# One fused decoder layer on one core: turned blocks stored whole, decays in two halves, exchanged banks, a third q,k buffer

## The chip, the core and the metric

The kernel runs on one core of a Trainium2 chip. The metric is the time of one execution on the device in microseconds (us). Three timed runs of the kernel before gave 1155.07, 1157.92 and 1158.22 us, so the median is 1157.92 us. One further execution was recorded by the profiler; all durations below are from it.

## What is computed

One decoder layer for 1024 rows of 1024 columns, in float32. With `h` the normed input, one projection gives q, k, v, z_a, a low-rank gate, four convolution inputs and two merge gates. Cut to what matters here:

```python
gk  = log_sigmoid(gk_low @ w_gk2 + b_gk) / 16          # decays
o   = gla_chunked(q, k, v, gk)                         # o_t = q_t S_t ; S_t = exp(gk_t) S_{t-1} + k_t^T v_t
y_a = (rms_norm(o, gla_norm_g) * silu(z_a)) @ w_branch_a
y_c = (cb * causal_dwconv(cc * xc) * silu(z_c)) @ w_branch_c
merged = sigmoid(g_a + b_ga) * y_a + sigmoid(g_c + b_gc) * y_c
x = x + merged @ w_out
x = x + sigmoid(rms_norm(x) @ w_ple_gate) * (p @ w_ple_proj)
out = rms_norm(x)
```

There are 4 heads with 128 key columns and 256 value columns, in chunks of 64 rows.

## The kernel before, in words

**Products.** Every float32 operand is split into a rounded high part and a low remainder, and a product is three matmuls (`mm3`, L604). The large products are 2 by 2 block products with seven block multiplications instead of eight (products 0 to 6, banks called X, Y and V). A `Cell` (L721) is one such product on one column block of weights; `wide` (L1061) is the form for v and z_a, with four banks at a time: X on `first`, V on `second`, Y on `first` again (L1120). The fourth bank of each four is one of two rotating buffers under the tag `o`, which other work uses too. `resident` (L637) splits the operand that stays in SBUF, one of seven slots `r0` to `r6`.

**Order.** Nothing is issued at once. `Flow.note` (L271) records every operation with a modelled cost, `set_dues` (L368) works out due times backwards, and `put_in_order` (L415) places the operations one by one: on each engine the one that can start first, by due time where several can. Large matmuls go in the order of the program; matmuls of side work (decays, attention) go in between as soon as their data are modelled to be there. What comes out is a fixed order for each engine, and an engine waits at an instruction whose data are late. All DMAs go out on SP's queue, in order. Buffers of one tag are handed out in program order; a pool made `instead` of another opens when the old one's last user is done. Side work is written as generators woven in by `weave` and `tick` (L612 to L623): a generator is resumed after so many ticks, two ticks for each four k-tiles.

**Stages, in the order of time.** Preparation of h and the first gate products; v and the decays; z_a; q and k; the convolution products; the gates (`ga`, `gc`) with the attention woven in; `yc`; `ya`; `out`; the last gate `gt` with the output.

- *Decays* (`decays`, L1169): a generator that runs beside v. For each half of the rows: a low-rank product into an `o` buffer, then for each head a matmul `zp` into an `o` buffer, then exp, log, a subtraction and a scan on tile `c` (tag `c4`, 2 buffers), stored as `cd`.
- *q, k* (`q_cons`, `k_cons`): scaled q and k go to DRAM (`qkd`). One k form is transposed in 32 by 32 blocks into `turned` and stored by `put_blocks` (L864) with four DMAs of 32 partitions each, so that DRAM holds the finished transpose (`ked`).
- *Attention* (`attend`, L1378): for each pair of heads eight row blocks and one closing step. A step's matmuls are one bundle: the state's growth `kv` and the output `op` of block s-1, then the scores `X` of block s. The loads of block s+1 (`fetch`, L1392: `qk`, `v`, `sz`, each behind its reader) come after step s; `qk` and `v` have two buffers each. `read_attended` (L1432) norms `op`, multiplies by `sz`, transposes, and after four blocks stores `od`, again by four DMAs.
- *Reload* (`switch`, L1492): the conv result `ud` and the attention result `od` are loaded (`uq`, `oq`) and split into resident operands. Pool `sw`, in which `uq` lies, opens `instead` of the attention's pool `att`.
- *Out and gate*: `flip` (L1600) transposes each half row block of x and stores it as `gd`, four DMAs each; `gt` cells load it as `raw`.

Of the kernel before, what the change touches and what calls it, by code (L numbers as in the profile page):

```python
# [49 lines left out]
class View:  # L50
# [88 lines left out]
    def place(self):  # L139
        real = self.buf.get()  # L140
        if self.apart:
            start, dims = self.apart
            return bass.AP(tensor=real.tensor, offset=real.offset + start,
                           ap=[[self.buf.size, 32]] + [[s, n] for s, n in dims])
# [113 lines left out]
class Flow:  # L258
# [12 lines left out]
    def note(self, engine, op, call, args, kw):  # L271
# [28 lines left out]
        elif engine == ACT:  # L300
            o.cost = 0.10 + n * 0.000833 + (0.1 if "accum_out" in kw else 0.0)
            o.table = TABLE.get(args[2] if len(args) > 2 else None, 0)
        elif engine == POOL:
            o.cost = 0.1 + n * 0.001 if op == "memset" else 0.6
        else:
            o.cost, o.bytes = 0.4, shape[0] * n * 4
            o.lat = 2.0 + o.bytes / 250e3
# [206 lines left out]
def kernel(  # L514
# [42 lines left out]
    vec = cp.tile([P, 62], F32, name="vec")  # L557
# [8 lines left out]
    ggla = vec[:, 60:62]  # L566
# [10 lines left out]
    ked = [[dram(f"ked{hp}_{i}", 2, 4 * P) for i in range(2)] for hp in range(2)]  # L577
# [9 lines left out]
    gd = [[dram(f"gd{p}_{q}", 2, 4, P) for q in range(2)] for p in range(4)]  # L587
# [49 lines left out]
    def resident(name, k, src):  # L637
        hi, lo = slot(k, "h", f"{name}{k}hi"), slot(k, "l", f"{name}{k}lo")
        for c in range(2):
            cs = slice(2 * c, 2 * c + 2)  # L640
            split(hi[:, cs, :], lo[:, cs, :], src[:, cs, :])
# [222 lines left out]
    def put_blocks(dst, start, dims, src):  # L864

        store(dst.spread(start, dims), src)


# [192 lines left out]
    def wide(name, w, pool, cons):  # L1061
# [49 lines left out]
        def copies(what, acc, tags):  # L1111
            out = []
            for b in range(4):
                where, tag = tags[b]
                t = where.tile([P, 512], F32, tag=tag, name=f"{name}{what}{b}", bufs=2)
# [4 lines left out]
        first, second = ("m0", "m1", "m2", "o"), ("m3", "m4", "m5", "o")  # L1120
        near = [(bp, "u2"), (bp, "u2"), (bp, "s5"), (bp, "s5")]
# [4 lines left out]
        x0 = copies("x", X, near)  # L1126
# [10 lines left out]
        c22 = copies("s", V, [(bp, "s5"), (bp, "s5"), (pool, "ws"), (pool, "ws")])  # L1137
        prep(5)
        product(2, Y, False)
        c12 = copies("u", Y, [(bp, "u2"), (bp, "u2"), (pool, "wu"), (pool, "wu")])  # L1140
# [14 lines left out]
    with phase("v", [ph["prep0"]]) as qp:  # L1155
# [13 lines left out]
        def decays():  # L1169

            smask = qp.tile([P, HALF], F32, name="smask")
            nc.gpsimd.memset(smask, 1.0)
            nc.gpsimd.memset(smask.rearrange("p (c t) -> p c t", t=CH)[:, :, 0:1], 0.0)
            graw = qp.tile([P, 8, 16], F32, name="graw")
            load(graw, wgl)
            gdif = qp.tile([P, 4, 16], F32, name="gdif")
            tt(gdif, graw[:, 4:8, :], graw[:, 0:4, :], op=ALU.subtract)


            glw = qp.tile([P, 12, 4, 32], F32R, name="glw")  # L1180
            for i in range(4):
                split(glw[:, 0:8, i, 0:16], glw[:, 0:8, i, 16:32], graw)
                split(glw[:, 8:12, i, 0:16], glw[:, 8:12, i, 16:32], gdif)
            g2raw = qp.tile([P, 512], F32, tag="low", name="g2raw")
            load(g2raw, wgk2)
            g2 = qp.tile([P, 512], F32R, name="g2")
            nc.scalar.copy(g2, g2raw)
            tt(g2[64:128], g2raw[64:128], f(g2[64:128]), op=ALU.subtract)
            yield 1
            for half in range(2):  # L1190

                ops = ((0, 0), (4, 3)) if half == 0 else ((0, 1), (8, 6))
                lowp = pso.tile([P, 512], F32, tag="o", name=f"lowp{half}", bufs=2)
                n = 0
                for g0, k in ops:
                    for kt in range(4):
                        gl = glw[:, g0 + kt, :, :].rearrange("p a b -> p (a b)")
                        for s in range(2):
                            mm(lowp, gl, hres[k][s][:, kt, :], start=n == 0, stop=n == 15)
                            n += 1  # L1200
                low = qp.tile([P, 512], F32R, tag="low", name=f"low{half}")
                nc.scalar.copy(low, lowp)
                for a in (32, 96):
                    tt(low[a:a + 32], lowp[a:a + 32], f(low[a:a + 32]), op=ALU.subtract)
                yield 1
                for hp in range(2):
                    t1 = qp.tile([P, 2, HALF], F32, tag="t1", name=f"t1_{half}{hp}")
                    c = [qp.tile([P, HALF], F32, tag="c4", name=f"c4_{half}{hp}{i}", bufs=2) for i in range(2)]
                    for i in range(2):
                        h = 2 * hp + i  # L1210
                        zp = pso.tile([P, 512], F32, tag="o", name=f"zp{half}_{h}", bufs=2)
                        cs = slice(h * P, (h + 1) * P)
                        mm(zp, g2[:, cs], low, start=True, stop=True)
                        act(t1[:, i, :], zp, AF.Abs, bias=bgk[:, h:h + 1])
                        nc.vector.tensor_scalar(c[i], zp, bgk[:, h:h + 1], 0.0, op0=ALU.add, op1=ALU.min)
                        yield 1
                    act(t1, t1, AF.Exp, scale=-1.0)
                    act(t1, t1, AF.Ln, bias=1.0)
                    for i in range(2):
                        tt(t1[:, i, :], t1[:, i, :], c[i], op=ALU.subtract)  # L1220
                        nc.vector.tensor_tensor_scan(c[i], smask, t1[:, i, :], 0.0, op0=ALU.mult, op1=ALU.add)
                        store(cd[2 * hp + i][half], c[i])
# [11 lines left out]
    with phase("qk", [ph["v"]]) as qp:  # L1234
# [36 lines left out]
        def k_cons(hp):  # L1271

            def cons(i, j, src):
# [104 lines left out]
    def attend(hp, ap):  # L1378
# [7 lines left out]
        ins, turns, aTs = {}, {}, {}  # L1386
        kes = slot(3, "h", f"ke{hp}", (2, 2, 512), F32)
        for i in range(2):
            load(kes[:, i], ked[hp][i])
        vb, qb = slot(0, "h", f"v{hp}", (2, 1024)), slot(0, "l", f"qk{hp}", (2, 1024))  # L1390

        def fetch(s):  # L1392
            v = vb[:, s % 2].rearrange("p (h l d) -> p h l d", h=2, l=2)
            qk = qb[:, s % 2].rearrange("p (h c) -> p h c", h=2)
            load(f(qk), qkd[hp][s // NP][:, s % NP])
# [8 lines left out]
            ins[s] = qk, v, sz, ke  # L1404

        def grow(s, kv):
            v = ins[s][1]
            for h in range(2):
                mm3(kv[:, h], *(k[:, h] for k in ins[s][3]), v[:, h, 0], v[:, h, 1], True, True)

        def attended(s, op):
            qk, v = ins[s][0:2]
# [19 lines left out]
        def read_attended(s, op):  # L1432
            sz = ins.pop(s)[2]
# [5 lines left out]
            nc.gpsimd.tensor_tensor(r, r, mhalf[:, 0:1].to_broadcast([P, 2]), op=ALU.pow)  # L1439
            for h in range(2):  # L1440
                stt(sz[:, h], op[:, h], r[:, h:h + 1], sz[:, h], op0=ALU.mult, op1=ALU.mult)
# [9 lines left out]
        for s in range(2):  # L1451
            fetch(s)
        yield 2
        for s in range(n + 1):
# [8 lines left out]
            if X:  # L1463
                qk = f(ins[s][0])
# [9 lines left out]
            if s and s + 1 < n:  # L1474
                fetch(s + 1)
            yield 3
# [15 lines left out]
    def switch(cell, name, side, pool, src, res, bufs=3, gain=None):  # L1492


        def get(n):
            t = pool.tile([P, 4, 512], F32, tag="f", name=f"{name}q{n}", bufs=bufs)
            load(t, src[n])
            if gain is not None:
                for kt in range(4):
                    act(t[:, kt, :], t[:, kt, :], AF.Copy, scale=gain[:, kt % 2:kt % 2 + 1])  # L1500
# [4 lines left out]
        def put(k, t):  # L1505
            res[k] = resident(name, k, t)
# [45 lines left out]
    def aq(d):  # L1552
        return [d[0][0], d[1][0], d[1][1], d[0][1]]
# [6 lines left out]
    with phase("sw", [ph["att"]]) as pool:  # L1560
# [5 lines left out]
        switch(ycs[3], "o", "A", pool, aq(od), ores, gain=ggla)  # L1566
# [14 lines left out]
    with phase("late", [ph["sw"], ep]) as lp:  # L1581
        flipped, rgate = set(), {}

        def make_out(p, cell):
# [47 lines left out]
        gts = [Cell(f"gt{p}", "A", [gd[p][n // 2][:, n % 2] for n in range(4)], gres, None, mixed=True) for p in range(4)]  # L1632
# [113 lines left out]

# [42 lines left out]
```

## Time and profile before

| | us |
|---|---|
| median of three timed runs | 1157.92 |
| profiled execution, whole time | 1154.9 |
| its span (first to last instruction) | 1153.1 |
| TensorE (PE) matmul busy | 1087.9 |
| VectorE (DVE) busy | 873.8 |
| ScalarE (ACT) busy | 586.4 |
| GpSimd (POOL) busy | 48.0 |

The span is what the recorded instructions cover; the whole time is 1.8 us longer. A view of windows gives, for stretches of the span, the busy time of each engine with its count of instructions in brackets, then the clock granted to TensorE (PEclk, 1.00 is full speed), the share of time in which the 16 DMA engines were busy, and the bytes moved per second. A view of waits adds up the idle time of an engine ahead of an instruction by what released it. The chain is the work that ended last, followed back. `SPq` is the issue of DMAs on SP's queue. All instructions carry the line of one helper, L502, so they are told apart by the names of their tiles.

### The profile page before, as it was taken

To read this page: it belongs to the slowest core of one execution; us is meant where nothing else is said; L and a number is where in the kernel's file an instruction comes from. 1 tells how busy PE (TensorE), PEld (TensorE's weight loads), DVE (VectorE), ACT (ScalarE), POOL (GpSimd) and SP (SyncE) were. 2 spreads that over 40 slices of the span, in tenths; PEclk is the share of its full clock that TensorE was granted. 3 is DMA by queue.
4 is the path that set the end of the run, shared out by engine and by line. 5 is a ranking of instruction groups with operands and counts; after the bars stand their busy time and mean duration, and the time that the engine had idled before them with its cause. 6 is when DMAs were issued, how large, how long until landed. Compare 5 with 4: busy or idle time off the path is not lost.

```text
span 1153.1 us, 14771 instructions
## 1 busy us (share of the span) xinstructions
PE 1087.9 (94%) x4893; PEld 896.8 (78%) x4893; DVE 873.8 (76%) x1359; ACT 586.4 (51%) x1037; POOL 48.0 (4%) x89
## 2 busy tenths in 40 slices
PE   8999498999999999999999999999499999998986
PEld 6877386888888888888888888887378888887875
DVE  6996556457987986956757687787499978887786
ACT  6766643546654346333333365565275725365554
POOL 0000000000000000000000011111000000011122
PEclk9999699999999999999999999999699999999999
DMA  8762247135876588421122769886667778788964
GB/s 319 232 227 95 74 154 254 68 127 179 257 231 198 195 284 278 149 87 61 61 85 65 267 219 309 292 276 200 208 240 257 272 246 286 249 285 274 300 234 159
DMA packets 150781, 237.87 MB, mean 206 GB/s; under 512 B 13232, under 2 KB 66736, under 8 KB 147632
## 3 DMA queue, kind: packets, MB, share of 16 engines
q1 hardware_dynamic: 150704, 236.93, 61.8%
q8 instruction: 38, 0.62, 0.2%
q14 instruction: 39, 0.32, 0.1%
HBM read 156.14 MB, written 80.74 MB: 205 GB/s over the span
## 4 chain that ended last, share of the span: by engine, by line
PE 79%; DMA 8%; DVE 5%; ACT 3%; SPq 2%; issue 1%; POOL 0%; POOLq 0%; DVEq 0%; ACTq 0%
PE vY L502 3%; PE zaY L502 2%; PE zaX L502 2%; PE vV L502 2%; PE zaV L502 2%; PE op L502 2%; SPq L502 2%; PE vX L502 1%; PE pe L502 1%; DMA wtd<-wt 1%; PE kv L502 1%; DMA gt1raw<-gd 1%; DMA x<-in_x_dram 1%; DMA wgq<-wtd 1%; PE ga3Y L502 1%
## 5 line engine op out<-in xcount | busy, mean ns | idle before, releaser
L502 ACT ACTIVATE junk<-x 128x512 bf16<-128x512 f32 (+1 forms) x29 | 17.9, 616 | 27.0 <-DVE x L502 21.7
L502 DVE TENSOR_TENSOR wt<-wt 128x512 f32<-128x512 f32 x32 | 21.5, 684 | 0.2
L502 POOL MEMSET t<- 128x2 f32 x8 | 0.8, 99 | 481.6 <-DMA ked<-turned 281.2
L502 DVE SCALAR_TENSOR_TENSOR u<-t,vec,u 128x1024 f32<-128x1024 f32 x16 | 20.3, 1276 | 0.0
L502 ACT ACT_TABLE_LOAD x15 | 19.2, 1283 | 1.0 <-PEq L1778 0.7
L502 POOL TENSOR_SCALAR rg<-ms 128x1 f32<-128x1 f32 x8 | 7.5, 932 | 250.9 <-ACT junk L502 250.8
L502 PE MATMUL yc0X<-u0hi,yc0hi 128*128 128x512 f32 x4 | 2.7, 669 | 16.1 <-ACT u0hi L502 16.1
L502 DVE TENSOR_TENSOR t<-t,c 128x512 f32<-128x512 f32 x8 | 5.3, 689 | 16.0 <-ACT t L502 15.9
L502 ACT CAST S<-S 128x512 fp32r<-128x512 f32 x14 | 8.6, 618 | 13.7 <-PE op L502 13.7
L502 PE MATMUL vV<-v1hi,h1hi 128*128 128x512 f32 x16 | 7.4, 460 | 8.5 <-DVE c L502 8.5
L502 DVE SCALAR_TENSOR_TENSOR szl<-op,or,szl 128x256 f32<-128x256 f32 x32 | 14.0, 476 | 0.9 <-POOL or L502 0.9
L502 PE MATMUL op<-S,qk 128*128 128x256 f32 x84 | 14.5, 281 | 0.0
L502 PE MATMUL pe<-wpehi,pTlo 128*128 128x512 f32 x32 | 13.2, 412 | 1.4 <-DVE pTlo L502 1.4
L502 PEld LDWEIGHTS yc0X<-u0hi,yc0hi 128*128 128x128 f32 x4 | 1.3, 319 | 16.8 <-ACT u0hi L502 16.5
L502 ACT ACTIVATE junk<-op 128x256 bf16<-128x256 f32 x32 | 12.1, 378 | 3.8 <-PE op L502 3.7
L502 DVE TENSOR_TENSOR x<-x,pe 128x512 f32<-128x512 f32 (+1 forms) x17 | 11.1, 655 | 2.9 <-DMA x<-x2d 2.7
L502 PE MATMUL pe<-wpehi,pThi 128*128 128x512 f32 x32 | 13.3, 417 | 0.0
L502 PE MATMUL pe<-wpelo,pThi 128*128 128x512 f32 x32 | 13.0, 408 | 0.0
L502 ACT ACTIVATE oq<-oq,vec 128x512 f32<-128x512 f32 x20 | 13.0, 712 | 0.0
L502 PE MATMUL op<-v,aTh 128*128 128x256 f32 x64 | 12.6, 280 | 0.0
L502 DVE SCALAR_TENSOR_TENSOR S<-S,dds,kv 128x256 f32<-128x256 f32 x24 | 10.4, 475 | 2.3 <-PE kv L502 2.3
L502 PEld LDWEIGHTS op<-S,qk 128*128 128x128 f32 x84 | 11.9, 188 | 0.0
(2900 smaller groups left out, 4132.9 us busy)
## 6 DMA issues: line engine op xcount, KB each, us to landing
wtd<-wt SPq DMA_DIRECT2D x44, 256.0 KB, 3.8
wt<-in_wb_dram SPq DMA_DIRECT2D x8, 1024.0 KB, 7.0
qk<-qkd SPq DMA_DIRECT2D x16, 512.0 KB, 6.4
v<-vd SPq DMA_DIRECT2D x16, 512.0 KB, 5.6
wgq<-wtd SPq DMA_DIRECT2D x7, 1024.0 KB, 7.8
vraw<-in_wv_dram SPq DMA_DIRECT2D x20, 256.0 KB, 3.5
zaraw<-in_wv_dram SPq DMA_DIRECT2D x20, 256.0 KB, 3.4
uq<-ud SPq DMA_DIRECT2D x5, 1024.0 KB, 7.9
```

The lines of the kernel that those rows point to most:

```text
L502: o.call(*[place(a) for a in o.args], **{k: place(a) for k, a in o.kw.items()})
```

## The change

1. *Turned blocks.* `put_blocks` is gone. `turned`, `oT` and `gr` are each stored by one DMA of 128 partitions as they lie. The placing is done by the loads: `placed(src, run)` makes a source pattern with runs of 128 elements (for `ked` and `gd`) or 512 (for `od`). `ked` is kept in one tensor for each head, so that the attention loads it with four DMAs for a pair of heads instead of two. The rows of `w_branch_a` and `w_ple_gate` and the gains are permuted beforehand to match; the gain on `oq` is applied to 128-column slices over four groups. `turned` is transposed from columns four apart.
2. *Decays.* The generator takes one half of the rows. Half 0 is woven into v, half 1 into z_a. `c4` has four buffers; the copies of `wide` go to other tags.
3. *Banks.* The `o` buffer is the third of the four. z_a has its X and Y on the banks on which v had V, and its V on those on which v had X and Y.
4. *Attention.* `qk` has three buffers (the third is the free half of the state's slot) and a load of its own, two blocks ahead. A step yields 3, 3, 2 ticks in turn instead of 3. `op` is scaled by two ACT copies into `og`, and one DVE multiplication by `sz` takes the place of two fused DVE operations on `op`.

```diff
+    def placed(src, run):
+        return src.spread(0, [(run, P), (32 * src.buf.size, 4), (1, run)])
...
-        first, second = ("m0", "m1", "m2", "o"), ("m3", "m4", "m5", "o")
...
-        weave(decays(), 1)
-        wide("v", [wv[0, n] for n in range(4)], qp, v_cons)
+        weave(decays(0), 2)
+        wide("v", [wv[0, n] for n in range(4)], v_cons, ("m0", "m1", "o", "m2"), ("m3", "m4", "o", "m5"),
+             [(ep, "ev", 3)] * 2, [(ep, "ev", 3), (qp, "wu", 1)])
         finish_woven()
-        wide("za", [wv[1, n] for n in range(4)], qp, z_cons)
+        weave(decays(1), 1)
+        wide("za", [wv[1, n] for n in range(4)], z_cons, ("m3", "m4", "o", "m5"), ("m0", "m1", "o", "m2"),
+             [(qp, "vhi", 2)] * 2, [(qp, "vlo", 2)] * 2)
+        finish_woven()
...
-                                    kf[:, :, P:2 * P].rearrange("p n (b c) -> p n b c", c=32))
-                for g in range(4):
-                    put_blocks(ked[hp][i][:, j, g * P:g * P + P], j * 512 + g * P, [(32 * 1024, 4), (1, P)],
-                               turned[32 * g:32 * g + 32].rearrange("p b n c -> p b (n c)"))
+                                    kf[:, :, P:2 * P].rearrange("p n (c b) -> p n b c", c=32))
+                store(ked[hp][i][j], turned.rearrange("p b n c -> p b (n c)"))
...
+        qbs = [qb[:, 0], qb[:, 1], state[:, 2:4].rearrange("p a b -> p (a b)")]
+        def fetch_qk(s):
+            qks[s] = qbs[s % 3].rearrange("p (h c) -> p h c", h=2)
+            load(f(qks[s]), qkd[hp][s // NP][:, s % NP])
...
             for h in range(2):
-                stt(sz[:, h], op[:, h], r[:, h:h + 1], sz[:, h], op0=ALU.mult, op1=ALU.mult)
+                act(og[:, h], op[:, h], AF.Copy, scale=r[:, h:h + 1])
+            tt(sz, og, sz, op=ALU.mult)
...
-                for g in range(4):
-                    put_blocks(od[i][hp][:, :, g * P:g * P + P], g * P, [(512, 4), (32 * 2048, 4), (1, P)],
-                               turns[i][32 * g:32 * g + 32].rearrange("p (k b) n c -> p k b (n c)", b=4))
+                store(od[i][hp], turns[i].rearrange("p (f k) n c -> p f (k n c)", f=4))
...
-            if s and s + 1 < n:
+            if s + 2 < n:
+                fetch_qk(s + 2)
+            if s + 1 < n:
                 fetch(s + 1)
-            yield 3
+            yield (3, 3, 2)[s % 3]
...
-        switch(ycs[3], "o", "A", pool, aq(od), ores, gain=ggla)
+        switch(ycs[3], "o", "A", pool, aq(od, lambda t: placed(t, 512)), ores, gain=ggla)
...
-                for a in range(4):
-                    put_blocks(gd[p][j][:, i, a, :], i * 512 + a * P, [(32 * 1024, 4), (1, P)],
-                               g[32 * a:32 * a + 32].rearrange("p (b k) c -> p b (k c)", k=4))
+                store(gd[p][j][i], g.rearrange("p (b k) c -> p b (k c)", k=4))
...
-        gts = [Cell(f"gt{p}", "A", [gd[p][n // 2][:, n % 2] for n in range(4)], gres, None, mixed=True) for p in range(4)]
+        gts = [Cell(f"gt{p}", "A", [placed(gd[p][n // 2][n % 2], P) for n in range(4)], gres, None, mixed=True) for p in range(4)]
```

More of the change, by code (lines that the diff above doesn't have):

```diff
@@ L142, in place @@
             start, dims = self.apart
-            return bass.AP(tensor=real.tensor, offset=real.offset + start,
-                           ap=[[self.buf.size, 32]] + [[s, n] for s, n in dims])
+            return bass.AP(tensor=real.tensor, offset=real.offset + start, ap=[[s, n] for s, n in dims])
         if self.dtype != self.buf.dtype:
@@ L306, in note @@
             o.cost, o.bytes = 0.4, shape[0] * n * 4
+            if getattr(ins[0], "apart", None):
+                o.cost, o.bytes = 0.6, 1.4 * o.bytes
             o.lat = 2.0 + o.bytes / 250e3
@@ L586 @@
     x2d = [dram(f"x2d{b}", D) for b in range(8)]
[L587 removed]
+    gd = [[[dram(f"gd{p}_{q}_{i}", 4, P) for i in range(2)] for q in range(2)] for p in range(4)]
     wtd = [[dram(f"wtd{w}_{n}", 4, 512) for n in range(4 + 3 * w)] for w in range(2)]
@@ L1059, with wide @@
     nc.vector.tensor_scalar(ggla, ggla, float(P) ** -0.5, None, op0=ALU.mult)
-    def wide(name, w, pool, cons):
+    def wide(name, w, cons, first, second, more_s, more_u):
         raw, ring, keep = {}, {}, {}
@@ L1113, in copies @@
             for b in range(4):
-                where, tag = tags[b]
-                t = where.tile([P, 512], F32, tag=tag, name=f"{name}{what}{b}", bufs=2)
+                where, tag, n = tags[b]
+                t = where.tile([P, 512], F32, tag=tag, name=f"{name}{what}{b}", bufs=n)
                 nc.scalar.copy(t, acc[b])
@@ L1125, in wide @@
         product(0, X, True)
-        x0 = copies("x", X, near)
+        x0 = copies("x", X, u2 + s5)
         prep(1)
@@ L1167, in z_cons @@
             store(szd[j][i][:, b], t.rearrange("p (h d) -> p h d", h=2))
[L1169 to L1222, printed above, removed]
-                    yield 1
@@ new lines, with decays @@
+        for i in range(4):
+            split(glw[:, 0:8, i, 0:16], glw[:, 0:8, i, 16:32], graw)
+            split(glw[:, 8:12, i, 0:16], glw[:, 8:12, i, 16:32], gdif)
+        g2raw = qp.tile([P, 512], F32, tag="low", name="g2raw")
+        load(g2raw, wgk2)
+        g2 = qp.tile([P, 512], F32R, name="g2")
+        nc.scalar.copy(g2, g2raw)
+        tt(g2[64:128], g2raw[64:128], f(g2[64:128]), op=ALU.subtract)
+        def decays(half):
+            ops = ((0, 0), (4, 3)) if half == 0 else ((0, 1), (8, 6))
+            lowp = pso.tile([P, 512], F32, tag="o", name=f"lowp{half}", bufs=2)
+            n = 0
+            for g0, k in ops:
+                for kt in range(4):
+                    gl = glw[:, g0 + kt, :, :].rearrange("p a b -> p (a b)")
+                    for s in range(2):
+                        mm(lowp, gl, hres[k][s][:, kt, :], start=n == 0, stop=n == 15)
+                        n += 1
+            low = qp.tile([P, 512], F32R, tag="low", name=f"low{half}")
+            nc.scalar.copy(low, lowp)
+            for a in (32, 96):
+                tt(low[a:a + 32], lowp[a:a + 32], f(low[a:a + 32]), op=ALU.subtract)
+            yield 2
+            for hp in range(2):
+                t1 = qp.tile([P, 2, HALF], F32, tag="t1", name=f"t1_{half}{hp}")
+                c = [qp.tile([P, HALF], F32, tag="c4", name=f"c4_{half}{hp}{i}", bufs=4) for i in range(2)]
+                for i in range(2):
+                    h = 2 * hp + i
+                    zp = pso.tile([P, 512], F32, tag="o", name=f"zp{half}_{h}", bufs=2)
+                    cs = slice(h * P, (h + 1) * P)
+                    mm(zp, g2[:, cs], low, start=True, stop=True)
+                    act(t1[:, i, :], zp, AF.Abs, bias=bgk[:, h:h + 1])
+                    nc.vector.tensor_scalar(c[i], zp, bgk[:, h:h + 1], 0.0, op0=ALU.add, op1=ALU.min)
+                    yield 1
+                act(t1, t1, AF.Exp, scale=-1.0)
+                act(t1, t1, AF.Ln, bias=1.0)
+                for i in range(2):
+                    tt(t1[:, i, :], t1[:, i, :], c[i], op=ALU.subtract)
+                    nc.vector.tensor_tensor_scan(c[i], smask, t1[:, i, :], 0.0, op0=ALU.mult, op1=ALU.add)
+                    store(cd[2 * hp + i][half], c[i])
+                yield 2
@@ L1505, in put @@
         def put(k, t):
-            res[k] = resident(name, k, t)
+            res[k] = resident(name, k, t, gain is not None)
         def after_a(k):
```

66 lines of the change are left out of this document (39 added, 27 removed).

## The prediction

> **What bounds the kernel now.** The page first:
>
> ```profile
> span 1153.1 us, 14771 instructions
> ...
> PE 1087.9 (94%) x4893; PEld 896.8 (78%) x4893; DVE 873.8 (76%) x1359; ACT 586.4 (51%) x1037; POOL 48.0 (4%) x89
> ```
>
> TensorE is the bound: it idles for 65.2 us of the span, and no edit removes a matmul. Time can come only from that idle time and from matmuls at a lowered clock. The view of windows, with stretches cut where the idle time lies, says where they are:
>
> ```profile
> 115.00:145.00 30.00, 14.38 (x44) 9.98 (x43) 17.02 (x23) 19.36 (x24) 0.00 (x0) 0.66 0.21 77
> 145.00:190.00 45.00, 45.00 (x200) 37.24 (x200) 24.89 (x40) 19.51 (x34) 0.00 (x0) 1.00 0.53 174
> 190.00:205.00 15.00, 11.29 (x37) 8.44 (x36) 9.56 (x15) 4.06 (x7) 0.00 (x0) 0.77 0.83 272
> 205.00:650.00 445.00, 444.66 (x1962) 367.49 (x1961) 326.61 (x526) 200.91 (x358) 1.35 (x10) 1.00 0.49 157
> 650.00:804.70 154.70, 154.69 (x838) 133.75 (x837) 119.64 (x227) 84.08 (x195) 14.88 (x30) 1.00 0.82 270
> 804.70:830.00 25.30, 8.76 (x24) 6.47 (x24) 7.28 (x9) 4.47 (x8) 1.05 (x2) 0.60 0.70 240
> 830.00:850.00 20.00, 15.45 (x65) 11.73 (x64) 19.81 (x21) 15.02 (x20) 0.00 (x0) 1.00 0.34 119
> ...
> 1045.00:1100.00 55.00, 48.23 (x210) 39.00 (x209) 44.05 (x64) 31.01 (x60) 9.33 (x11) 1.00 0.91 293
> ```
>
> The first number is the length, then PE's busy time with its matmuls; the third from the end is the clock. From 205 to 650 us PE is never idle: 444.66 us for 1962 matmuls, 0.2266 us each. At that pace a stretch's matmuls are worth count times 0.2266; the rest of its length is lost, by idling or by the clock. (The few matmuls missing from a trace make such a loss slightly too large.)
>
> - 115 to 145 (v): 44 are worth 10.0; **20.0 lost**.
> - 190 to 205 (v to z_a): 37 are worth 8.4; **6.6 lost**.
> - 804.7 to 830 (`yc` begins): 24 are worth 5.4; **19.9 lost**; 830 to 850: 65 are worth 14.7; **5.3 lost**.
> - 1045 to 1100 (`out` to `gt`): 210 are worth 47.6; 7.4 lost.
>
> Who ends them, from the view of PE's waits (us, times, longest):
>
> ```profile
> PE yc0X L502 <- ACT u0hi L502: 16.1, 1, 16.1
> PE vV L502 <- DVE c L502: 8.5, 1, 8.5
> PE zaX L502 <- DVE vlo L502: 3.7, 2, 2.0
> PE gt0Y L502 <- DVE gt0s L502: 3.7, 1, 3.7
> PE zp L502 <- DVE vlo L502: 3.4, 1, 3.4
> PE zp L502 <- DVE low L502: 2.8, 1, 2.8
> PE vX L502 <- ACT vx L502: 2.7, 2, 1.9
> ```
>
> **Decays and banks.** In v, bank four of V is an `o` buffer, and in program order every `zp` and `lowp` of both halves comes before it. So V waits for the last decay: 8.5 on `c`, with 3.4 and 2.8 on the decay's own matmuls. The chain shows why `c` is late: its two buffers are reused, and the reuse waits for a store.
>
> ```profile
> 134.19 1.98 DMA cd<-c
> ...
> 137.07 11.30 PE vV L502 x39
> ```
>
> With four `c` buffers that store is waited for by nothing, and only half 0's five `o` users come before V. Its decay starts with X, and X's two products last some 22 us (96 matmuls at 0.2266) besides 3.7 us of the low-rank product; so a decay of one half, whose steps are of the size of that store, has the length of X to finish. I take the whole 20.0 as gone in v; the 2.7 of vX, waits for X's copies on a crowded ACT, stays. Half 1 meets the same rotation in z_a: sixteen `lowp` matmuls move there, at no net cost, but `zp` and V share two buffers, and exp and log load tables beside the copies. The nearest rows are vX's 2.7 and `zp`'s 3.4. Bounds of the new stalls in z_a: 0 to 12 (8.5 and 3.4 again); I take **3**, near vX, since `c` has buffers now.
>
> z_a's X now takes the banks of v's V, which were read before v's last product began; the wait of zaX on `vlo` (3.7) was for v's last Y. So the 6.6 goes: what is next, z_a's V on v's old X banks, comes some 22 us later. `ev`, `vhi` and `vlo`, which now also hold copies, are idle at those points.
>
> The clock is part of these sums: 0.66 and 0.77 in the rows above. The Trainium skill, "TensorE: Matmul & The Clock Gate", Part 1, says that PE falls to half rate after an idle window of about 3.4 us and comes back after as long a busy one. An estimate by that page is half of 3.4 us, 1.7, for each of the three holes, 5.1 in all. The rows give more (lost less idle: 4.4, 2.9 and 3.4 with 15.6, 3.7 and 16.5 idle, 10.7 in all); by the page's figure the forecast would be 5.6 later. The 3.7 before gt0Y lies in a stretch at 1.00, so a wait of that length need not cost clock, as the page's free-running window allows.
>
> **Attention.** The hole at 804.7 is the end of the attention with nothing left to run beside it:
>
> ```profile
> 811.73 7.93 DMA uq<-ud
> 819.68 1.05 ACT u0hi L502
> 820.76 1.24 DVE u0lo L502
> ...
> 822.04 5.06 PE yc0X L502 x11
> ```
>
> The last step's transpose is followed by the stores of `oT`; then `uq`, whose pool opens behind the attention, takes 7.93 us; and from 830 to 850 DVE makes the further u operands (19.81 busy of 20). PE has its last gate matmul at 804.7 (the window's edge). If the attention ended 16.1 us earlier, the hole would close; some 25 us earlier, the slow start would go too. What sets its pace?
>
> ```profile
> 683.81 0.61 PE L502 MATMUL X<-qk 128*128 128x128 f32 x4
> ...
> 799.20 0.61 PE L502 MATMUL X<-qk 128*128 128x128 f32 x4
> ```
>
> ```profile
> 674.42 0.38 SPq L502 DMA_DIRECT2D qk<-qkd  x1
> ```
>
> ```profile
> qk<-qkd SPq DMA_DIRECT2D x16, 512.0 KB, 6.4
> v<-vd SPq DMA_DIRECT2D x16, 512.0 KB, 5.6
> ...
> szl<-szd SPq DMA_DIRECT2D x16, 256.0 KB, 4.8
> od<-oT SPq DMA_DIRECT2D x16, 256.0 KB, 4.5
> ```
>
> These are timelines of PE (X is the last of a bundle) and SP, and the groups of DMA issues (the last column is the median from issue to landing). A `qk` load can go only when the bundle that read its buffer is through. This one goes at 674.42 and by its group's median lands 6.4 later, at 680.8. The bundle for which it is has 18 matmuls of 256 columns, half of 0.2266 each, 2.1 us, ahead of its X at 683.81: it begins at 681.7. So the load is in series with the step: 6.4 + 2.1 and about 1 for the hand-overs, 9.5. From 683.81 to 799.20 lie 13 steps, 8.9 us each. With three buffers a `qk` load has a whole step more, as `v` has now: twice the step, less 2.1, must hold 6.4 + 1, so a step may be 4.8. (Ticks do not pace it: a bundle goes when it is ready.)
>
> Then DMA is the limit. A step loads 512 + 512 + 256 KB, 1.31 MB; sixteen with `ke` (2.1 MB) and `od` (4.2) are 27.3 of the 41.8 MB that 154.7 us at 270 GB/s moved. That is 176 GB/s, and 94 for the rest. 270 at a share of 0.82 makes 329 at a full one. At 7.0 us a step the attention is some 25 us shorter: 27.3 MB in 130 us, 210 GB/s, and some 86 for the rest, since the gates get less of PE: 296, a share of 0.90. At 6.0 it would be 0.97. I take **7.0**, near the highest shares above: 13 × 1.9 = 24.7 us earlier, just enough for 25. I leave **3** of the 25.2 standing, and take **3** for bundles whose loads come late on a PE that goes in order (bounds 0 and, at 3 for each of 16 steps, 48).
>
> ```profile
> L502 DVE SCALAR_TENSOR_TENSOR szl<-op,or,szl 128x256 f32<-128x256 f32 x32 | 14.0, 476 | 0.9 <-POOL or L502 0.9
> ...
> L502 ACT ACTIVATE junk<-op 128x256 bf16<-128x256 f32 x32 | 12.1, 378 | 3.8 <-PE op L502 3.7
> ```
>
> Moved work: a step's DVE loses two fused operations of 0.476 and gains one multiplication of 512 columns (0.62, half of u0lo's 1.24 for 1024). ACT gains two reads of `op` of about 0.378 in 7 us, and is 84.08 busy of 154.70: hidden there. The two reads wait for POOL's `or`, a wait that DVE had and that cost it 0.9 in all (the first row); now the casts of the gates' weights queue behind it on ACT, and PE waits for those. ACT has half its time free, so I cost it at nothing; if that cover fails, 0.9 again. The closing chain grows by 0.4, inside the lead.
>
> **Turned blocks.** SP issues 48 + 24 + 12 stores fewer. In `out` and `gt` 64 stores (issue time in ns: least, median, most) share the queue with the loads that gt's operands wait for:
>
> ```profile
> L502 SPq DMA_DIRECT2D gd<-gr x64: 302/430/1637, 1009.7 to 1087.2; - x64
> ```
>
> 48 × 0.43 is 20.6 us of queue between 1010 and 1087. The runs of 512 bytes do not vanish; they go from stores to loads, and no row shows such a load. Bounds: all 7.4 of the stretch gained, or its waits doubled, 7.4 lost. I take **3 gained**: issue falls, bytes stay. The strided transpose of `turned` is eight operations where PE is never idle; hidden, or, if each takes 0.62 more, 5 us at most. `ke` comes in four loads of short runs instead of two; the first growth of each pair of heads waits for them, twice in all, inside the 3 for late loads.
>
> **Sum.** 1153.1 − (20.0 + 6.6 + 25.2) − 3 (turned) + 3 (z_a) + 3 (`yc`) + 3 (late loads) = 1107.3 of span; with the 1.8 us around it 1109.1. The profiled execution, 1154.9, lies 3.0 under the median of 1157.92; I put the median after at **1110**, one above the sum. Its own range: 1099 with none of the three costs of 3, 1118 with each doubled.
>
> **Rivals.**
>
> - *DMA holds the step at 8.* For: a share of 0.82 at 8.9. Against: 0.91 stands from 1045 to 1100. At 8.0 the lead is 12; of 25.2 some 13 stay, 10 more than taken: 1120. Chance 0.18.
> - *The third buffer changes nothing*: another wait (the state's chain through ACT and DVE, or `v`) holds the step at 8.9, and the change does not do there what it says. All 25.2 stay, less some 2 for three `od` issues ahead of `uq`: 1130. Against: the `v` arithmetic above. Chance 0.08.
> - *The decay's waits move to z_a whole*: 12 instead of 3, with the clock 4 more: 1123. Against: half the users, four `c` buffers. Chance 0.10.
> - *Slower: late loads on an in-order PE.* PE now never waits from 650 to 804.7 since bundles stand behind generous slack. Packed at the DMA's limit, each of 16 bundles may wait for `qk` or `v`. The gain of 48 is eaten at 3.0 us a bundle; at 4, a landing of 10 instead of 6, 64 us: 1171. Against: a late bundle is put off in the planner's order by the same modelled queue that had no stall before. Chance 0.05.
> - *No change*, from such waits at 2.8 us a bundle: 1155. Chance 0.02.
>
> **How the numbers follow.** The forecast keeps 0.57. The range 1099 to 1131 reaches over the first three rivals' times and leaves out the last two and both tails, under 0.2. About 0.3% is what a measurement of this kernel can tell from no change, 3.5 us. Faster: 0.57 + 0.18 + 0.08 + 0.10 = 0.93; same 0.02; slower 0.05.
>
> **What would show it.** Right: PE busy without a break through v and z_a at clock 1.00; `uq` loaded some 20 us before the last gate product ends; X of the attention every 7 us; 16 stores of `gr`. Wrong: a wait of zaV on `c` or `zp` over 4 us; `kv` or `X` waiting on a DMA again and again; yc0X waiting on u0hi over 5 us; gt matmuls waiting on `raw` longer than now.

## The result, and the profile after

The kernel after takes **1086.83 us** (median of four runs, 1086.27 to 1087.08) against 1158.07 for the kernel before on the same chip (four runs, 1155.07 to 1159.05): a ratio of 0.9388, 95% interval 0.9371 to 0.9406. The forecast was 1110.0, with a range from 1099 to 1131. The sign and the order of the parts were right; the gain, 71.2 us, is half as large again as the 48 that were forecast, and the time lies under the range.

The profiled execution took 1086.71. Its page begins:

```profile
span 1084.8 us, 14656 instructions
...
PE 1071.5 (99%) x4893; PEld 890.8 (82%) x4893; DVE 870.0 (80%) x1343; ACT 598.9 (55%) x1071; POOL 49.3 (5%) x89
...
PEclk9999999999999999999999999999999999999998
```

The same 4893 matmuls as before. The span is 68.3 shorter: PE's idle time went from 65.2 to 13.3 (51.9), and its busy time from 1087.9 to 1071.5 (16.4), chiefly since the clock is no longer lowered (the mean granted clock was 0.976 and is 0.997). All that PE still waits for, in the view of its waits, is this:

```profile
PE warm L503 <- DVE zero L503: 1.4, 1, 1.4
PE vV L503 <- DVE c L503: 1.2, 1, 1.2
PE zaX L503 <- ACT zax L503: 0.6, 1, 0.6
```

The rest of the 13.3 is the tail, 10.0 from the end of PE's last matmul to the end of the span. The view of windows for the stretches that were cut in the prediction (v; v's second half; the start of z_a; the attention; the end of the gates; the start of `yc`; `out` and `gt`):

```profile
76.00:103.00 27.00, 27.00 (x119) 22.08 (x118) 25.45 (x48) 18.15 (x33) 0.00 (x0) 1.00 0.36 122
103.00:163.00 60.00, 58.80 (x258) 48.03 (x257) 34.73 (x54) 30.82 (x51) 0.00 (x0) 1.00 0.54 180
163.00:178.00 15.00, 14.36 (x62) 11.16 (x61) 12.47 (x20) 9.75 (x15) 0.00 (x0) 1.00 0.71 229
...
650.00:735.00 85.00, 85.00 (x502) 75.21 (x501) 71.44 (x136) 60.34 (x156) 14.18 (x26) 1.00 0.91 315
735.00:770.00 35.00, 35.00 (x156) 29.00 (x155) 27.41 (x35) 21.41 (x33) 0.00 (x0) 1.00 0.79 278
770.00:795.00 25.00, 25.00 (x112) 20.67 (x112) 24.67 (x32) 20.01 (x32) 0.00 (x0) 1.00 0.77 279
975.00:1030.00 55.00, 55.00 (x244) 45.56 (x243) 48.12 (x69) 33.84 (x62) 8.82 (x10) 1.00 0.96 318
```

Where the prediction read clocks of 0.66, 0.77 and 0.60 there is 1.00 in every row, and PE's busy time fills all but 1.8 us. Since the stages come in the same order in both kernels, the time of the first matmul of each name (timelines of PE) cuts both spans into the same pieces of work:

| from the first | before | after | gain | forecast |
|---|---|---|---|---|
| start to `vX` (preparation, first gates) | 82.34 | 76.22 | 6.1 | 0 |
| `vX` to `q0X` (v, z_a) | 192.86 | 164.99 | 27.9 | 23.6 |
| `q0X` to `ga0V` (q, k, convolution) | 382.03 | 381.30 | 0.7 | 0 |
| `ga0V` to `ya0X` (gates with attention, `yc`) | 249.52 | 223.47 | 26.0 | 19.2 |
| `ya0X` to `out0X` | 76.16 | 76.16 | 0 | 0 |
| `out0X` to PE's end (`out`, `gt`) | 160.57 | 152.63 | 7.9 | 3 |
| PE's end to the end | 9.62 | 10.03 | -0.4 | 0 |

So the 22.5 us between the forecast of the span and the span lie in four places: 6.1 in the start, which the prediction never looked at, 4.3 in v and z_a, 6.8 in the attention, 4.9 in `out` and `gt`. The attention itself, by a timeline (the second and the last `X` of the first pair of heads, the first and the last of the second pair; then the last store, the load of `uq` and the first cast of it):

```profile
635.25 0.61 PE L503 MATMUL X<-qk 128*128 128x128 f32 x4
...
669.28 0.61 PE L503 MATMUL X<-qk 128*128 128x128 f32 x4
...
682.11 0.60 PE L503 MATMUL X<-qk 128*128 128x128 f32 x4
...
723.22 0.61 PE L503 MATMUL X<-qk 128*128 128x128 f32 x4
...
733.57 0.33 SPq L503 DMA_DIRECT2D od<-oT  x1
739.25 2.51 SPq L503 DMA_DIRECT2D uq<-ud  x3
...
749.04 2.00 ACT L503 CAST u0hi<-uq 128x1024 fp32r<-128x1024 f32 x2
```

Six steps in 34.03, then seven in 41.11: 5.7 and 5.9 us each. The first operand of `yc` is cast at 749, and `yc0X` begins at 769.82. Where PE waited 16.1 before, there are some 19 us in hand. The groups of DMA issues (KB each, median us from issue to landing; `S<-qkd` is the third buffer, which lies in the state's slot):

```profile
v<-vd SPq DMA_DIRECT2D x16, 512.0 KB, 5.3
qk<-qkd SPq DMA_DIRECT2D x12, 512.0 KB, 5.5
...
od<-oT SPq DMA_DIRECT2D x4, 1024.0 KB, 8.2
gd<-gr SPq DMA_DIRECT2D x16, 256.0 KB, 4.7
...
S<-qkd SPq DMA_DIRECT2D x4, 512.0 KB, 6.0
```

### The profile page after: what moved, and what is told of

Read it like the earlier page. It is cut to its first block, busy times and chain, and to the rows that moved or that the text cites. A ratio compares the mean times of both kernels' runs of the same rounds, so it can differ in the third digit from the quotient of the medians.

```text
span 1084.8 us, 14656 instructions
## 1 busy us (share of the span) xinstructions
PE 1071.5 (99%) x4893; PEld 890.8 (82%) x4893; DVE 870.0 (80%) x1343; ACT 598.9 (55%) x1071; POOL 49.3 (5%) x89
## 4 chain that ended last, share of the span: by engine, by line
PE 96%; DVE 1%; ACT 1%; issue 1%; POOL 0%; DMA 0%; POOLq 0%; DVEq 0%; ACTq 0%
PE vY L503 3%; PE zaY L503 3%; PE pe L503 2%; PE zaV L503 2%; PE op L503 2%; PE vV L503 2%; PE zaX L503 2%; PE kv L503 1%; PE vX L503 1%; PE ga2Y L503 1%; PE ga0Y L503 1%; PE ga1Y L503 1%; PE ga3Y L503 1%; PE gc1Y L503 1%; PE cb3Y L503 1%; PE gc0Y L503 1%
## 5 line engine op out<-in xcount | busy, mean ns | idle before, releaser
L503 ACT ACTIVATE junk<-x 128x512 bf16<-128x512 f32 (+1 forms) x29 | 17.9, 616 | 19.0 <-DVE x L503 16.1
L503 ACT ACTIVATE og<-op,or 128x256 f32<-128x256 f32 x32 | 13.3, 469 | 1.7 <-POOL or L503 1.7
L503 ACT ACTIVATE oq<-oq,vec 128x512 f32<-128x512 f32 x20 | 13.3, 716 | 0.0
L503 POOL TENSOR_TENSOR or<-or,mhalf 128x2 f32<-128x2 f32 x16 | 12.7, 795 | 1.3
L503 PE MATMUL op<-v,aTh 128*128 128x256 f32 x64 | 12.6, 280 | 0.0
L503 PE MATMUL pe<-wpelo,pThi 128*128 128x512 f32 x32 | 12.6, 394 | 0.0
L503 DVE TENSOR_TENSOR szl<-og,szl 128x512 f32<-128x512 f32 x16 | 11.0, 686 | 1.7 <-ACT og L503 1.7
L503 DVE SCALAR_TENSOR_TENSOR hq<-hq,vec,rt 128x512 f32<-128x512 f32 x16 | 11.0, 744 | 1.0 <-PE rt L503 1.0
L503 DVE STREAM_TRANSPOSE oT<-szl 128x512 f32<-128x512 f32 x16 | 11.3, 705 | 0.2
L503 DVE TENSOR_TENSOR u<-u,s 128x512 f32<-128x512 f32 x16 | 10.9, 689 | 0.3
L503 DVE SCALAR_TENSOR_TENSOR x<-x,rf,gfin 128x1024 f32<-128x1024 f32 (+2 forms) x8 | 8.9, 1113 | 2.7 <-POOL rf L503 2.7
```

The costliest lines, as they stand in the source:

```text
L503: o.call(*[place(a) for a in o.args], **{k: place(a) for k, a in o.kw.items()})
```

## The experiments

**The theory**: the change removes four independent losses, one in each place of the table, and each has one part of the change behind it; the terms of the prediction were right in kind and taken too small. **The rivals**: one part does most of it and the others matter little; or the parts need each other; for the start, that the order of the first loads did it. Each kernel ran beside the kernel before on the same chip, which took 1156.32 us beside the first four, 1154.83 beside the next four and 1156.18 beside the last four. The kernel after was timed in its own group alone, and the kernel before moved by up to 3.2 us between the groups (1154.83 to 1158.07). So a difference from the kernel after is also read from the stages of the traces, where it can be told which stage it lies in.

### Undoing one part of the kernel after

**q,k in two buffers**, the load behind its reader again:

```diff
-        qbs = [qb[:, 0], qb[:, 1], state[:, 2:4].rearrange("p a b -> p (a b)")]
+        qbs = [qb[:, 0], qb[:, 1]]
...
-            if s + 2 < n:
-                fetch_qk(s + 2)
+            if s and s + 1 < n:
+                fetch_qk(s + 1)
```

> The changed kernel with the q,k loads back in two buffers, each load behind its reader; all else as changed. Theory (the qk load was in series with each attention step): a step takes about 9 us again, the attention ends with the gate products, yc0X waits some 14 to 16 us on u0hi, and the time goes from 1086.8 to between 1106 and 1112. Rival (the whole stores and the fewer DMA issues closed the hole, not the buffer): step near 6 to 7, no wait at yc0X, 1086 to 1090.

1109.81, 23.0 over the kernel after; `X` comes every 9.3 us (634.72 to 765.54, 14 steps), and the waits show the old hole and the slow start behind it:

```profile
PE yc0X L503 <- ACT u0hi L503: 13.3, 1, 13.3
...
PE yc0V L503 <- ACT u1hi L503: 1.4, 1, 1.4
PE yc0X L503 <- DVE u3lo L503: 1.3, 1, 1.3
```

All other stages are as in the kernel after within 0.6 us. The load in series with the step was the limit.

**The turned blocks** stored by four DMAs each again (`ked`, `od` and `gd`, with the loads and the row order that belong to them):

```diff
-                store(gd[p][j][i], g.rearrange("p (b k) c -> p b (k c)", k=4))
+                for a in range(4):
+                    put_blocks(gd[p][j][:, i, a, :], i * 512 + a * P, [(32 * 1024, 4), (1, P)],
+                               g[32 * a:32 * a + 32].rearrange("p (b k) c -> p b (k c)", k=4))
```

> The changed kernel with the three transposed blocks stored by four DMAs of 32 partitions again and loaded as they lie; all else as changed. Theory (these stores cost SP's queue and little else): out and gt lose 3 to 7.6 us again, the attention stays fast: 1090 to 1096. Rival (the short stores held the DMA engines and with them the attention): steps of 8 us and more, a wait at yc0X on u0hi, 1100 or more. The start up to the first gate product stays at 30.4 us if it does not hang on these blocks.

1096.24, 9.4 over, more than the 3 to 7.6 that were expected, nearly all of it in `out` and `gt` (2.7 before `gt0X`, 6.2 from there to `gt2X`).

**Both halves of the decays beside v**, with the new banks and four `c` buffers:

```diff
-        weave(decays(0), 2)
+        def whole():
+            yield from decays(0)
+            yield from decays(1)
+        weave(whole(), 2)
...
-        weave(decays(1), 1)
```

> The changed kernel with both halves of the decays woven into v, one after the other; four c buffers, third-bank o and exchanged banks stay. Theory (V stands behind every zp in the rotation of o): vV waits on c again, 8 to 18 us in v, so 1095 to 1105; and if the due times of half 1 also pushed the early loads about, the first gate product moves from 30.4 back to about 36.6 us: then 1101 to 1111. Rival (the four c buffers or the bank order were enough): vV waits under 3 us, 1086 to 1090.

1099.47, 12.6 over: v 14.9 longer, z_a 2.4 shorter, the start 0.7 longer. PE's waits:

```profile
PE vY L503 <- ACT vY L503: 4.0, 1, 4.0
PE zp L503 <- ACT t L503: 3.4, 1, 3.4
PE zp L503 <- ACT vhi L503: 2.0, 1, 2.0
```

No wait on `c` is among them, so the time lies in the expected range, but not for the expected reason: with four buffers and an `o` that is not V's last bank, the decay's own products and v's copies wait for a crowded ACT instead. In z_a the same half costs 2.4; four `zp` matmuls at 0.2266 make 0.9 of that and the wait of `zaX` 0.6, and the rest is not accounted for. The low-rank product of half 1 is no part of it: in the kernel after its 16 `lowp` run among v's last matmuls. What the start gained does not come from the halving.

**z_a on the banks of v**, in the same order:

```diff
-        wide("za", ..., z_cons, ("m3", "m4", "o", "m5"), ("m0", "m1", "o", "m2"),
+        wide("za", ..., z_cons, ("m0", "m1", "o", "m2"), ("m3", "m4", "o", "m5"),
```

> The changed kernel with z_a on the same banks in the same order as v. Theory: zaX waits on vlo again, about 3.7 us idle and 2.9 us of lowered clock, 1092 to 1095. Rival (half a decay less beside v leaves v's last stores early enough): no wait of zaX, 1086 to 1088.

1103.30, 16.5 over, more than twice what was expected:

```profile
PE q0V L503 <- DVE sz L503: 5.4, 1, 5.4
PE zp L503 <- DVE c L503: 3.0, 1, 3.0
PE zaX L503 <- DVE vlo L503: 2.0, 1, 2.0
...
PE zp L503 <- DVE vlo L503: 0.7, 1, 0.7
```

The wait of `zaX` on `vlo` is the one that the prediction took away (3.7 there, 6.6 with the clock); with the waits of `zp` behind it z_a is 8.6 longer. But q (`q0X` to `k0X`) is 8.0 longer too: its first V stands on a bank, `m2`, that z_a's consumers, `sz`, still read. The kernel before does not have this wait (q takes 19.2 there and 19.0 in the kernel after). There `m2` is the third bank that `sz` reads; with `o` moved to the third place it is the last. So the new place of `o` brings this collision, and the exchange takes it away again. Neither the prediction nor the expectation had looked one stage further.

### One part alone on the kernel before

**v and z_a alone** (decays in halves, banks, `c` buffers, tags):

> The kernel before with only the part on v and z_a (decays in two halves, banks, c buffers, tags). Theory (the parts gain in stages of their own and add up): start 6.2, v and z_a 27.9 less, all else as before, so 34 under before: 1121 to 1126. Rival (part of what v and z_a gain is given back later, or needs the other parts): 1130 or more. If the start's 6.2 come from another part: 1128 to 1131.

1121.31, 33.5 under the kernel before: the start 5.8 shorter, `vX` to `q0X` 27.6. The theory's sum holds. The attention's hole stands as before (15.5 on `u0hi`).

**The attention's part alone**:

> The kernel before with only the attention's part (third q,k buffer, ticks, two copies of op on ACT). Theory: the gates with the attention and yc gain 26.0, the start nothing: 1130 to 1134. Rival (the turned blocks stored whole take part in it, by fewer issues and other loads): 1137 or more.

1129.85, 25.0 under and at the lower edge of what was expected; `ga0V` to `ya0X` is 223.47 long, to the hundredth as in the kernel after, with the turned blocks of before. They take no part in it.

**The turned blocks alone**:

> The kernel before with only the turned blocks stored whole. Theory (undoing this part in the kernel after cost 9.4, all of it in out and gt): 8 to 12 under before, 1145 to 1150, of which 0 to 2 in the hole at yc by three fewer issues of od. Rival (the 3 of the prediction is the part's own, the rest is only there in the kernel after): 1153 to 1156.

1143.75, 11.1 under, a little more than expected: 7.9 in `out` and `gt` by the stages, as in the whole change, and 3.3 in the hole at `yc`, where one issue of `od` stands ahead of `uq` instead of four (3.23 us in the kernel before). Within the whole change that hole is closed already, so there they are worth nothing.

The three parts alone are worth 33.5, 25.0 and 11.1, together 69.6, of which the 3.3 in the hole at `yc` can't count twice. The stages say it more closely than the times: 5.8 and 27.6, 26.0, and 7.9 make 67.3 of the 68.3 by which the span is shorter. So they add up; no part needs another, and none is given back later. The theory had four losses with a part for each. The runs show four losses and three parts: the start and v with z_a hang on the same one. Within that part the halves and the exchange were undone alone; the four `c` buffers, the new place of `o` and the tags of the copies were not.

### What the start's six microseconds come from

In the kernel before the second pair of `pTraw` loads goes out behind six and seven of the eight loads of `hq`; in the kernel after, behind one and two. The first idea was that order:

```diff
+        nc.hurry = -16.0
         get_x(1)
+        nc.hurry = 0.0
```

> The kernel before; only the loads of the second half of h are wanted 16 us later by the planner, so that the second pair of pT loads goes out ahead of them. Theory (the 6.2 of the start come from this order alone, which the decays' earlier dues had set): 1150 to 1153, first gate product 5 to 6.5 earlier. Rival (the order of loads is a by-product, and the start gains by the smaller work beside it): 1156 to 1159.

1156.51, ratio 1.0017 (1.0002 to 1.0032): the idea falls. The first gate product does come 5.9 earlier, but `vX` does not:

```profile
PE gc1pX L502 <- DVE gc1plo L502: 2.6, 1, 2.6
...
PE gc1pX L502 <- DVE pe L502: 1.2, 1, 1.2
```

The loads of h's second half were late, but the work on them was still wanted early, so DVE took it up as soon as it could and the gates' weights stood behind it. The wait of 1.2 ends at 59.7 us, that of 2.6 at 74.1. From 44 to 60 us the groups of DVE are led by

```profile
L502 DVE TENSOR_TENSOR hq<-hq,hq 128x1024 f32<-128x1024 f32 x6 | 7.1, 1218 | 0.0
L502 DVE SCALAR_TENSOR_TENSOR hq<-hq,vec,rt 128x512 f32<-128x512 f32 x8 | 5.4, 740 | 0.0
```

which is 12.5 of 16 us. The stall only moved.

The two runs that follow change nothing but the **pace at which the decays' generator is resumed**, which says where its operations stand in the order of the program. In the kernel before, every step a third as often:

```diff
-            yield 1
+            yield 3
```

> The kernel before; the decays' generator is resumed a third as often (each yield 1 is a yield 3), nothing else. Theory (its pace decides how many of the decays stand ahead of v's V in program order, and by the due times how early the second half of h is wanted): the start gains its 6, v a part of its 20: 1129 to 1143. Rival (two halves with c buffers of their own and banks are needed, and the start has another cause): 1148 or more.

1138.23, a ratio of 0.9850 (0.9797 to 0.9904): **18 us by one number**. The start is 6.3 shorter, `vX` to `zaX` 12.0, z_a 0.4 longer. The order of PE's instructions in the two programs, with their count, shows what moved (16 `lowp` begin a half):

```
before:  vX(10) lowp(16) vX(18) zp vX(10) zp vX(10) zp vX(39) zp vX(9) vV(1) lowp(16) vV(8) zp zp zp zp vV(39) vY(48) vV(48) vY(96)
yield 3: vX(43) lowp(16) vX(15) zp vX(8) zp vX(10) zp vX(20) vV(19) zp vV(29) vY(48) vV(48) vY(11) lowp(16) vY(17) zp vY(8) zp vY(8) zp vY(52) zp
```

The second half has slid behind V by itself. Its waits:

```profile
PE zaX L502 <- DVE vlo L502: 6.2, 2, 4.1
...
PE vV L502 <- DVE vlo L502: 4.0, 1, 4.0
PE zp L502 <- DVE c L502: 2.1, 1, 2.1
```

And the other way round, in the kernel after with both halves beside v, where the generator's longer steps become short:

```diff
-            yield 2
+            yield 1
...
-                yield 2
+                yield 1
```

> The kernel after with both halves beside v (as in the run at 1099.5), but with each step of the generator a tick apart instead of two after the first and the last step of a half. Theory: the start goes back to some 31, so 5 slower than that run: 1103 to 1108. Rival (start not set by the pace): 1098 to 1101.

1104.61, 5.1 over the run with the longer steps; the stage from the first `pe` to `ga0pX` is 30.36 instead of 25.71 (before 31.13, after 24.97). So the pace sets the start, in both directions. How it does so is read from the code, and no run shows it. One of V's banks is an `o` buffer, buffers go in program order, and due times are worked backwards. What stands ahead of V in the program must be done before V, and what it reads, the second half of h, becomes due early, in the stretch where PE waits for `pT`. But standing ahead of V is not enough. In `wide` a tick comes after every second block, eight for each four k-tiles, so X lasts 16. The `lowp` of half 1 are resumed at the 9th of these in the kernel before and in this run, and at the 12th in the run at 1099.5: ahead of V in all three, yet there the start is only 0.7 longer than in the kernel after. So how early they stand matters too, and the exact link stays open.

### Which stores, and what else of the attention

**Only `gr` by four DMAs again** in the kernel after (the diff above, without `ked` and `od`):

> The kernel after with only gr stored by four DMAs again (gd), ked and od whole. Theory (the 9.4 of all three lie in the 48 stores of gr): 1094 to 1098. Rival (ked and od share it): 1088 to 1092.

1096.90, as much as with all three undone, so the whole of the 9.4 is in the stores of `gr`. SP's timeline of this run, and then of the kernel after, at the same place of the work:

```profile
986.75 1.27 SPq L503 DMA_DIRECT2D gt1raw<-gd  x2
...
989.37 0.49 SPq L503 DMA_DIRECT2D gt1raw<-gd  x1
991.24 10.72 SPq L503 DMA_DIRECT2D gd<-gr  x12
1002.00 1.44 SPq L503 DMA_DIRECT2D x2d<-x  x3
```

```profile
991.07 1.83 SPq L503 DMA_DIRECT2D gd<-gr  x3
992.94 4.64 SPq L503 DMA_DIRECT2D x2d<-x  x5
...
1000.68 0.37 SPq L503 DMA_DIRECT2D gt2raw<-gd  x1
```

Twelve stores hold the queue for 10.72 us, 0.89 each; three hold it for 1.83. What stands behind them, the rest of x and the loads of `raw`, comes later, and `gt0Y` waits 5.4 for DVE in that run. Whether the queue or the DMA engines behind it made the twelve issues slow, no run separates. The other price that the prediction weighed, loads in runs of 512 bytes, can be read in the groups of issues of the kernel after:

```profile
gt0raw<-gd SPq DMA_DIRECT2D x4, 256.0 KB, 5.5
gt1raw<-gd SPq DMA_DIRECT2D x4, 256.0 KB, 6.0
gt2raw<-gd SPq DMA_DIRECT2D x4, 256.0 KB, 5.4
gt3raw<-gd SPq DMA_DIRECT2D x4, 256.0 KB, 7.1
```

The kernel before has 7.0, 7.6, 5.5 and 5.5 there: on the whole no dearer.

**Only the third buffer** of the attention's part (ticks and copies of `op` undone):

```diff
-            yield (3, 3, 2)[s % 3]
+            yield 3
...
-                act(og[:, h], op[:, h], AF.Copy, scale=r[:, h:h + 1])
-            tt(sz, og, sz, op=ALU.mult)
+                stt(sz[:, h], op[:, h], r[:, h:h + 1], sz[:, h], op0=ALU.mult, op1=ALU.mult)
```

> The kernel after with the ticks and the two copies of op undone, so that of the attention's part only the third q,k buffer is left. Theory (the step is set by the q,k loads and the DMA alone): 1086 to 1089. Rival (the copies on ACT or the closer ticks shorten the step): 1091 or more.

1087.03, 0.2 from the kernel after, which a measurement can't tell from none. The steps take 5.7 and 5.8 us, against 5.7 and 5.9 in the kernel after. The buffer is the whole of the attention's gain; ACT's copies and the closer ticks are worth nothing, as the prediction costed them.

No version that ran beats the kernel after. What the waits leave is 1.8 us in v and z_a, and the tail of 10.0 is a chain that none of the parts touches.

## Why the prediction fell short, step by step

- *PE is the bound, and only idle time and a lowered clock can go*: right; both went nearly whole. But the losses were looked for from 115 us on. **The first 85 us were never cut into windows.** There stood 2.4 us of waits ahead of the first gate product, 1.4 at `gc1pX`, and 1.7 of lowered clock, most of the 6.1 us that the start lost to work which runs 60 us later, the decays. The prediction treated weaving as a matter of where the woven work runs. Its pace can also move a stall far ahead of that work; by the code, through how early the inputs are wanted.
- *v, 20.0 gone*: right but for 1.2, the wait of `vV` on `c` that is left. *"the 2.7 of vX stays"*: wrong, vX waits for nothing after; with fewer decays beside it ACT is less crowded, as the run with both halves beside v shows from the other side. *z_a's new stalls, 3*: mis-sized; they measure 0.6. *Sixteen `lowp` move to z_a*: they do not, they run among v's last matmuls. *The 6.6 by the banks*: right, and with `o` in the third place the exchange is needed for q as well, by the 8.0 that q loses without it.
- *The step of the attention*: the mechanism (the q,k load in series with the step; a third buffer takes it out) is shown by the two runs at 1109.81 and 1087.03. Two sizes were wrong. The step before is **9.6, not 8.9**: the prediction counted the 13 rows of `X` from 683.81 to 799.20 as 13 steps, and they are 12. Its own sum of 9.5 for the series, from the landing time and the bundle, was the better number, and the difference should have been a warning. And the step after is 5.7 to 5.9, not 7.0. So from `ga0V` to the last `X` it is 100.7 instead of 142.0: a lead of 41, where 25 were needed and 24.7 forecast. With that, *3 left of the 25.2* and *3 for late loads* measured 0 each: PE never waits for `qk`, `v` or `u`.
- *DMA as the limit, at a share of 0.97 for steps of 6.0*: the share from 650 to 735 is 0.91 at 315 GB/s, 346 at a full one, where the prediction scaled from 329. The share of busy time is not a fixed price per byte. The rival that DMA holds the step at 8 falls with it; so do the one of late loads on an in-order PE and the one that the buffer changes nothing.
- *Turned blocks, 3*: mis-sized; 7.9 in the stages, 9.4 when undone. The step that failed is the one that took the 20.6 us of queue as an even thinning, at a median issue of 0.43. A median hides the slow ones: by SP's timeline the 64 stores of the kernel before hold the queue for 45.3 us, and the 16 after for 7.3. The stores that matter go out twelve in a row, at 0.85 to 0.89, ahead of the loads of the next operands, and PE then waits. The strided transpose and the four loads of `ke` were rightly costed at nothing: `q0X` to `ga0V` did not grow, and PE waits for no `ke`.
- *The decays' waits move to z_a whole*: fell. With half 1 there z_a is 2.4 longer than without.

Three costs that were taken at 3 measured 0.6, 0 and 0, and the gain taken at 3 measured 7.9: four cautious terms, 13 us together. With the 2.7 of `vX` and the 6.1 of the start they are the miss. The range was built around them; its lower end, 1099, was "none of the three costs" (three times 3 off the sum of 1109.1 is 1100, not 1099), and left the turned blocks at 3 and the start at 0.

## What to carry to other kernels

When PE is the bound and a kernel loses time in holes, cut the whole span into windows, the first stage too, and price every hole with its clock; where each hole has its own cause, the gains add up. In a kernel whose order a planner works out, the pace at which side work is woven in can cause a stall far ahead of where that work runs: changing the pace by one number is a cheap test. A median issue time says nothing of stores that go out in a row; read the queue's timeline where they do. Check a step time that is counted from rows against the one that its chain adds up to, before either goes into a sum.

## What the hardware showed that was not expected

A lowered clock needs no long wait. In the kernel before the three waits of PE around 20 us are short (view of waits up to 45 us), and yet the clock falls (view of windows):

```profile
PE pe L502 <- DVE pTlo L502: 1.4, 1, 1.4
PE ms L502 <- DVE sq L502: 0.8, 1, 0.8
PE rt L502 <- DVE rb L502: 0.2, 1, 0.2
```

```profile
22.00:23.00 1.00, 0.76 (x4) 0.50 (x4) 0.98 (x2) 1.00 (x2) 0.00 (x0) 0.64 1.03 358
23.00:24.00 1.00, 1.00 (x5) 0.75 (x3) 1.00 (x2) 0.52 (x2) 0.00 (x0) 0.50 0.81 291
24.00:25.00 1.00, 1.00 (x4) 0.68 (x3) 1.00 (x3) 0.92 (x2) 0.00 (x0) 0.50 0.91 303
25.00:26.00 1.00, 1.00 (x5) 0.76 (x4) 1.00 (x2) 0.00 (x0) 0.00 (x0) 0.66 0.50 170
```

The 2.4 us of waits between 17 and 22.5 us cost 1.7 more by the clock (0.36, 0.50, 0.50 and 0.34). The Trainium skill, "TensorE: Matmul & The Clock Gate", Part 1, says that the clock is halved after one idle window of about 3.4 us and comes back after a busy one of that length; by that page of the Trainium skill one such fall costs an estimated 1.7. The amount agrees here. The condition, read as one unbroken idle stretch of that length, does not: no idle piece was longer than 1.4, and PE was idle for under half of those 5.5 us; sixteen of its matmuls between the waits were those of `ms`, one column wide (1.92 us). A fall can also hold on for longer: in the hole before z_a of the kernel before, two waits of 2.0 and 1.7 put the clock at 0.50 from about 196.4 to 203.2, for 6.8 us. In all, PE's busy time fell by 16.4 us, most of it the holes' clock, beside 51.9 of idling.
